# First modulations partly on VectorE, gate products of the next pair in between, stores by two queues

## The chip, the cores and the metric

The kernel runs on one core of a Trainium2 chip. The metric is device time in microseconds (us) of one execution; times of several runs are given as their median. One execution was recorded by the hardware profiler. Engines: PE is TensorE (PEld its weight loads), DVE VectorE, ACT ScalarE, POOL GpSimd, SP SyncE, which issues most DMAs.

## The reference

One layer with shared weights for 1024 latent tokens and 256 context tokens, width 1024, all in float32. `c` and `c_ctx` give nine modulation vectors each (shift, scale, gate for three sublayers):

```python
mods = split(silu(c) @ w_ada + b_ada, 9)
mods_c = split(silu(c_ctx) @ w_ada + b_ada, 9)
h  = ffn_sublayer(h, mods[0..2], g_ffn1, w_ffn1_in, w_ffn1_out)        # h + 0.5*gate*((silu(a)*b) @ w_out)
hc = ffn_sublayer(hc, mods_c[0..2], ...)                               # the context, the same weights
p_lat, p_ctx = project(h, ...), project(hc, ...)                       # q k v gates | o u vs ga gb
...                                                                    # mLSTM over chunks in both directions
mixed = sigmoid(ga) * (y_a @ w_a) + sigmoid(gb) * (y_b @ w_b)
h = h + mods[5] * (mixed @ w_o)
h = ffn_sublayer(h, mods[6..8], g_ffn2, w_ffn2_in, w_ffn2_out)
out = rmsnorm(h, g_final)
```

Each sublayer's input is `rmsnorm(h, g) * (1 + scale) + shift`.

## The kernel before

A float32 operand is split into two fp32r halves, hi (a cast on ScalarE, L143) and lo (a subtraction on VectorE, L144), and each product is three matmuls: hi hi, hi lo, lo hi. The large products of the latent stream save further by schemes of seven products where a plain block product needs eight (classes Gate, Out and others); they need sums of weight blocks and of activation blocks ahead of the products, on GpSimd (`presum`, L355 and L356, L371 to L374) and VectorE.

A scheduler in the builder sets the order of each engine's instructions; it starts from the order of the code and may let a step pass another whose buffer comes free later. Steps that are off the main line are put in a list `todo`; after each group of matmuls `pump` takes from it as many steps as the credit of the issued columns pays for. A step costs 512 unless it says otherwise, and an empty step `nop` is a way to let time pass. Buffers come from pools by a tag; a new tile of a tag takes the place of an older one and waits for the last reader of that. Tags `pg0` and `pg1` have eight pages each and serve one stage after the other.

The start: `vec`, a first part of `cst`, 32 pages of `w_ada` and `hc` (the context, two loads) are issued by SyncE in one row. The first two modulations (shift and scale of the first FFN) are computed in four quarters of 256 columns. Quarter qt holds the two slices d = 2qt and 2qt+1 of each modulation; `ada_mm` accumulates it by eight matmuls (tile adr), `ada_out` copies the row, turns it into columns (adc) and adds the bias (mods), and `scale_mod` gives smod. `nct` is the norm of the context: squares, `rstd` (p, then 11 small steps rs_x, rs_y, rs_z and diag), `bcast` (rb, a matmul that spreads the rows) and per d `mod0` (nt, hnc). Then come 22 blocks f of the context's first FFN, with two weight loads (raw, halves hl) per block, 24 matmuls pa and 24 pb each. In the first ten of them the latent stream is loaded (h), gets its position term (`add_pos`), is stored (hsp) and its squares are summed (acc on VectorE; p, L201, on TensorE). Later modulations are computed on VectorE: L751 multiplies a page by a scalar and adds, STREAM_TRANSPOSE (adtr) and TENSOR_REDUCE (adred) sum over partitions.

`Gate` computes the first half of an FFN for the latent stream: products 1 to 7 of each block pair f, in the order of `self.steps`. `head` pairs (three) run interleaved ahead of the others (order HSEQ, the last one is p=3), the other pairs overlap by two. A product of one pair over 512 columns is 12 matmuls (qa or qb by fa, fb or fc, and ring, the ring of split weights). The copy `p<-qa` (L404) and the steps L406 to L438 take the products out.

The merge: `load_split` and `last_y` put y_b and y_a into pages yp, `w_b` and `w_a` use them, fin_a forms m (gt<-gt,pt L1933, then m L1934), and the split of m is mx, in pages `pg{tb}`, for w_o. SyncE loads the next FFN's weights (rawh) meanwhile, and B.head starts their sums.

At the end `put` scales the normed output, on GpSimd where `pool_`, else on VectorE, and each result is stored at once (L1986).

Of the kernel before, what the change touches and what calls it, by code (L numbers as in the profile page):

```python
# [23 lines left out]
NKT = D // 128  # L24
# [31 lines left out]
def _build(ctx, tc, nc, a, out):  # L56
# [48 lines left out]
    class Weights:  # L105
# [10 lines left out]
        def load(self):  # L116
            n, i, w = self.order.popleft()
            src = a[n][i]
            if self.n % 4 < 2:
                raw = self.pool.tile([128, w], F32, name="raw", tag="raw", bufs=2)  # L120
            else:
                raw = hnp.tile([128, w], F32, name="raw", tag="pg1", bufs=8)
            self.n += 1
            nc.sync.dma_start(raw, src)
            hl = self.pool.tile([128, 2, w], F32R, name="hl", tag="hl", bufs=3)
            split(hl, raw)
            self.ready.append((n, i, hl))
            self.held += 1
# [44 lines left out]
    def wk(hl, k, w=128, o=0):  # L173
        return hl[:, 0, o + k * w:o + (k + 1) * w], hl[:, 1, o + k * w:o + (k + 1) * w]

    def proj(pt, wl, pgs, first):
        mm3(pt, [wk(wl, k) + (pgs[k][:, 0, :], pgs[k][:, 1, :]) for k in range(NKT)], first)

# [137 lines left out]
    class Gate:  # L316


        def __init__(self, name, raw, ring, depth, sums, pairs, head):
            self.name, self.raw, self.ring, self.depth, self.sums, self.pairs = name, raw, ring, depth, sums, pairs  # L320
            fs = [f for kp in range(pairs) for f in (kp, kp + pairs)]
            self.head = fs[:head]
            self.steps = [(f, p) for p in HSEQ for f in self.head]
            rest = fs[head:]
            for n, f in enumerate(rest):
                g = rest[n - 1]
                if not n:
                    self.steps += [(f, p) for p in (1, 2, 6, 5, 7)]
                else:
                    self.steps += [(f, 1), (f, 5), (g, 4), (f, 6), (g, 3)]  # L330
                    self.steps += [(f, p) for p in ((7, 2) if f == rest[-1] else (2, 7))]
# [465 lines left out]

    def ada_pages(qt):
        pages = []
        for kp in range(NKT // KP):  # L800
            pg = hnp.tile([128, KP, 2, QW], F32, name="adapg", tag=f"pg{1 - qt // 2}", bufs=8)
            for i in range(KP):
                src = a["w_ada"][kp * KP + i].rearrange("p (m c) -> p m c", m=9)[:, 0:2, qt * QW:(qt + 1) * QW]
                nc.sync.dma_start(pg[:, i], src)
            pages.append(pg)
        return pages

    def ada_mm(pages):
        pr = sm_ps("adr")
        for k in range(NKT):  # L810
            T.matmul(pr[0:2, 0:2 * QW], sc2[:, :, k], pages[k // KP][:, k % KP].rearrange("p m c -> p (m c)"),  # L811
                     start=k == 0, stop=k == NKT - 1)
        return pr

    def ada_out(qt, pr):
# [7 lines left out]
        for q in range(2):  # L823
            V.tensor_add(mods[:, 0:2, q, sl],
                         pc[:, 0:4 * QD].rearrange("p (m d q) -> p m d q", m=2, q=2)[:, :, :, q], bv[:, 0:2, sl])
            scale_mod(0, 1, q, "g_ffn1", sl)

    smod = cp.tile([128, 3, 2, 8], F32, name="smod")
# [34 lines left out]
    for _ in range(10):  # L863
        T.matmul(junk[:, 0:128], ones, ones, start=True, stop=True)
    apg = [ada_pages(0)]
    load_c(hcp, 4)
    for qt in (1, 2, 3):
        apg.append(ada_pages(qt))
    nc.sync.dma_start(cst[:, 1:], a["cst"].rearrange("p (a b) -> p a b", a=5)[:, 1:])
    nc.sync.dma_start(pos, a["pos"])  # L870
    hncp = [fxpage("hnc", F32R, (128, 2, 2, 256)) for _ in range(4)]
# [5 lines left out]

    prs = [ada_mm(apg[0])]
    for d in range(NKT):
        nct.sq(d)  # L880
    prs.append(ada_mm(apg[1]))
    nct.rstd()
    for qt in range(NQ):
        ada_out(qt, prs[qt])
        if qt < 2:
            prs.append(ada_mm(apg[qt + 2]))
        if qt == 0:
            nct.bcast()
        if qt:
            W.load()  # L890
        for d in range(qt * QD, (qt + 1) * QD):
            mod0(d)

# [8 lines left out]
    for f in range(NF):  # L902
        if f < NKT:
            for tb in range(2):
                nc.sync.dma_start(h[tb][f], a["xT"][f, :, tb * 512:(tb + 1) * 512])
        if 2 <= f < 2 + NKT:
# [474 lines left out]
    hnc = [fl("hnc", "hnc", (128, 2, 256), F32R, 8) for _ in range(NKT)]  # L1381
    nct.queue(smod[:, 1, 1, :], mods[:, 3, 1, :], hnc, gap=(1, 2, 12), cost=1280)
    nkq = pair_steps(("wk", emit_kq(ksp, 8), emit_kc), ("wq", emit_kq(qsp, 0)))
# [356 lines left out]
    def load_split(dst, src, tb, k):  # L1740
        r_ = t2("ld")
        nc.sync.dma_start(r_, src[tb, k])
        dst[tb][k] = hnpage(k // 4, "yp")
        split(dst[tb][k], r_)
# [124 lines left out]
    def last_y(hf, ct, sg):  # L1869
        ya[hf][ct] = hnpage(ct // 4, "yp")  # L1870
        split(ya[hf][ct], sg)
# [105 lines left out]
    n1_ = n3[1]  # L1977
    B.gate([n1_.rstd] + [nop] * 3 + [n1_.bcast] + B.F.late(fpage, lambda k: [lambda: n1_.inplace(k, m7, m6)]))

    def put(n_, tb, d, pool_, cs=slice(0, 512)):  # L1980
# [3 lines left out]
        else:  # L1984
            V.scalar_tensor_tensor(o_, o_, vc("g_final", d), n_.rb, ALU.mult, ALU.mult)
        nc.sync.dma_start(out[d, :, tb * 512 + cs.start:tb * 512 + cs.stop], o_)  # L1986

# [106 lines left out]
```

## Time and profile before

| | us |
|---|---|
| median of 3 runs | 2686.34 (2681.06 to 2689.07) |
| profiled execution | 2682.41 |
| its span | 2680.3 |
| VectorE busy | 1916.7 (72%) |
| ScalarE busy | 1141.7 (43%) |
| GpSimd busy | 440.6 (16%) |
| mean DMA rate | 170 GB/s |

The chain of work that ended last is 89% TensorE, 6% VectorE, 2% issue and 1% DMA. TensorE's idle time is thus what an edit can change, unless it changes the number of matmuls. In rows of the timeline a bracket gives the idle time of the engine just before the row and what ended it; `xN` is the number of instructions that stand in one row.

### The profile page before, as it was taken

To read this page: it belongs to the slowest core of one execution; us is meant where nothing else is said; L and a number is where in the kernel's file an instruction comes from. 1 tells how busy PE (TensorE), PEld (TensorE's weight loads), DVE (VectorE), ACT (ScalarE), POOL (GpSimd) and SP (SyncE) were. 2 spreads that over 40 slices of the span, in tenths; PEclk is the share of its full clock that TensorE was granted. 3 is DMA by queue.
4 is the path that set the end of the run, shared out by engine and by line. 5 is a ranking of instruction groups with operands and counts; after the bars stand their busy time and mean duration, and the time that the engine had idled before them with its cause. 6 is when DMAs were issued, how large, how long until landed. Compare 5 with 4: busy or idle time off the path is not lost.

```text
span 2680.3 us, 35678 instructions
## 1 busy us (share of the span) xinstructions
PE 2650.2 (99%) x12754; PEld 2210.3 (82%) x12754; DVE 1916.7 (72%) x3243; ACT 1141.7 (43%) x1952; POOL 440.6 (16%) x422
## 2 busy tenths in 40 slices
PE   9999999999999999999999999999999999999998
PEld 5998888888889878888888888888887788888887
DVE  4897688686979646687664868677568766675855
ACT  4664444344336525564443443121245444344432
POOL 0041333220000210000002005342102323230000
PEclk9999999999999999999999999999999999999999
DMA  8842344369578222356553467448140332337645
GB/s 299 315 173 99 142 165 149 114 217 327 156 254 281 85 79 86 106 169 199 194 176 105 140 238 268 166 167 279 58 159 24 126 140 99 135 122 274 201 157 173
DMA packets 202240, 456.73 MB, mean 170 GB/s; under 512 B 20432, under 2 KB 54480, under 8 KB 202064
## 3 DMA queue, kind: packets, MB, share of 16 engines
q1 hardware_dynamic: 202064, 454.47, 49.6%
q8 instruction: 100, 1.64, 0.3%
q14 instruction: 76, 0.62, 0.1%
HBM read 328.95 MB, written 125.51 MB: 170 GB/s over the span
## 4 chain that ended last, share of the span: by engine, by line
PE 89%; DVE 6%; issue 2%; DMA 1%; ACT 1%; SPq 0%; POOL 0%; POOLq 0%; ACTq 0%; DVEq 0%
PE pq L1240 17%; PE qa L389 17%; PE po L508 14%; PE qb L389 12%; PE pt L1719 9%; PE pr L1159 6%; PE pc L1030 2%; PE pn L1832 2%; PE pu L1559 2%; PE pa L169 1%; PE pb L169 1%; PE pkc L1219 1%; PE adr L811 1%; PE pn L1830 1%; DVE h L292 1%
## 5 line engine op out<-in xcount | busy, mean ns | idle before, releaser
L144 DVE TENSOR_TENSOR ring<-rawq,ring 128x512 fp32r<-128x512 f32 x408 | 310.6, 762 | 204.9 <-ACT ring L143 202.2
L508 PE MATMUL po<-gring,wring 128*128 128x512 f32 (+1 forms) x1896 | 425.1, 385 | 0.5 <-DMA gring<-fsp 0.5
L508 PEld LDWEIGHTS po<-gring,wring 128*128 128x128 f32 x1896 | 349.5, 188 | 71.9 <-issue 1.0
L143 ACT CAST ring<-rawq 128x512 fp32r<-128x512 f32 x408 | 252.9, 621 | 299.5 <-PE pq L1240 82.1
L389 PE MATMUL qa<-fc,ring 128*128 128x512 f32 x1056 | 252.6, 390 | 2.3 <-DVE ring L144 1.4
L389 PEld LDWEIGHTS qa<-fc,ring 128*128 128x128 f32 x1056 | 198.1, 188 | 44.2 <-DVE ring L144 1.8
L1240 PE MATMUL pq<-fc,ring 128*128 128x512 f32 x864 | 207.8, 393 | 0.0
L143 ACT CAST wring<-rw 128x512 fp32r<-128x512 f32 x154 | 95.9, 622 | 228.3 <-PE po L508 220.9
L1240 PEld LDWEIGHTS pq<-fc,ring 128*128 128x128 f32 x864 | 161.6, 188 | 33.3
L1719 PE MATMUL pt<-yp,ring 128*128 128x512 f32 x768 | 183.9, 396 | 1.2 <-ACT ug L1297 1.2
L144 DVE TENSOR_TENSOR wring<-rw,wring 128x512 fp32r<-128x512 f32 x154 | 106.3, 691 | 93.9 <-ACT wring L143 93.7
L1719 PEld LDWEIGHTS pt<-yp,ring 128*128 128x128 f32 x768 | 144.2, 188 | 30.7 <-ACT ug L1297 1.4
L1240 PE MATMUL pq<-fa,ring 128*128 128x512 f32 x576 | 142.3, 395 | 0.0
L1240 PE MATMUL pq<-fb,ring 128*128 128x512 f32 x576 | 138.2, 394 | 0.0
L389 PE MATMUL qa<-fb,ring 128*128 128x512 f32 x528 | 128.6, 394 | 3.7 <-ACT p L404 3.7
L389 PE MATMUL qa<-fa,ring 128*128 128x512 f32 x528 | 127.7, 391 | 1.2 <-DVE ring L144 0.7
L389 PE MATMUL qb<-fb,ring 128*128 128x512 f32 x528 | 126.8, 390 | 1.2 <-DVE p L406 0.6
L1240 PEld LDWEIGHTS pq<-fb,ring 128*128 128x128 f32 x576 | 107.7, 188 | 23.7 <-issue 0.2
L389 PE MATMUL qb<-fa,ring 128*128 128x512 f32 x528 | 126.2, 389 | 0.0
L389 PE MATMUL qb<-fc,ring 128*128 128x512 f32 x528 | 126.2, 389 | 0.0
L751 DVE SCALAR_TENSOR_TENSOR adacc<-adapg,sc,adacc 128x512 f32<-128x512 f32 x140 | 111.4, 814 | 20.1 <-DMA adapg<-in_w_ada_dram 19.3
L1240 PEld LDWEIGHTS pq<-fa,ring 128*128 128x128 f32 x576 | 106.9, 188 | 22.5 <-DVE ring L144 0.2
(342 smaller groups left out, 4803.9 us busy)
## 6 DMA issues: line engine op xcount, KB each, us to landing
adapg<-in_w_ada_dram SPq DMA_DIRECT2D x144, 256.0 KB, 3.7
fsp<-fhl SPq DMA_DIRECT2D x66, 512.0 KB, 2.6
gring<-fsp SPq DMA_DIRECT2D x66, 512.0 KB, 4.2
raw<-in_w1i_dram SPq DMA_DIRECT2D x44, 512.0 KB, 5.5
graw<-fsp SPq DMA_DIRECT2D x88, 256.0 KB, 3.6
rawq<-in_w1i_dram SPq DMA_DIRECT2D x38, 512.0 KB, 3.4
rawq<-in_w2i_dram SPq DMA_DIRECT2D x38, 512.0 KB, 3.6
fsp<-p SPq DMA_DIRECT2D x66, 256.0 KB, 2.1
```

Source lines behind the costliest of these rows:

```text
L143: S.copy(hl[:, 0, :], src)
L144: V.tensor_sub(hl[:, 1, :], src, hl[:, 0, :].bitcast(F32))
L169: T.matmul(pt, x, y, start=first and i == 0, stop=i == n - 1, skip_group_check=True)
L389: T.matmul(pt, hl[:, x, sl], pages[p][k][:, y, :], start=first and i == 0, stop=i == 11, skip_group_check=not first)
L508: T.matmul(pt[:, cs], w[:, x, sl], g[:, y, cs], start=grp and kp == 0 and i == 0, stop=kp == NFP - 1 and i == 2, skip_group_check=not grp)
L751: eng.scalar_tensor_tensor(acc, pgt, sc2[:, q, k:k + 1], acc, ALU.mult, ALU.add)
L1030: T.matmul(pt, hl[d // 4][:, x, sl], g[:, y, :], start=f == 0 and d % 2 == 0 and i == 0, stop=f == NF - 1 and i == 2, skip_group_check=True)
L1159: T.matmul(self.pt[m], pg[:, x, sl], hl[:, y, :], start=first and k == 0 and i == 0, stop=k == 3 and i == 2, skip_group_check=not first)
L1240: T.matmul(pt, hl[:, x, k * 128:(k + 1) * 128], pg[k][:, y, :], start=first and k == 0 and i == 0, stop=k == 3 and i == 2, skip_group_chec ...
L1559: T.matmul(pu[:, 0:257], ksl[:, kt * 128:(kt + 1) * 128], wv, start=True, stop=True)
L1719: T.matmul(pt, hl[:, x, k * 128:(k + 1) * 128], pg[:, y, :], start=kh + k + i == 0, stop=kh == 1 and k == 3 and i == 2)
L1832: T.matmul(pn[:, 0:257], qi[:, c_, :], self.C[d][:, c_, :], start=False, stop=c_ == 1)
```

## The change

Start: quarter 3 (d=6,7) is summed on VectorE (`ada_side`, accumulators adacc, transposes, reduces, a small matmul), the others stay on TensorE. Its pages are loaded in turn with those of quarter 1, and quarter 2's come last. The product of the context's FFN goes through k in the order 0,1,2,3,6,7,4,5. Most of `cst` and all of `pos` are loaded after the first weight loads, each h one block later. Gates: products 1, 2 and 6 of the first pair after the heads stand between the heads' products 3. Three counts of empty steps change, pages pg0 and pg1 of y_a and y_b are exchanged, and the last three results of GpSimd are stored by ScalarE's queue.

```diff
     def proj(pt, wl, pgs, first):
-        mm3(pt, [wk(wl, k) + (pgs[k][:, 0, :], pgs[k][:, 1, :]) for k in range(NKT)], first)
+        mm3(pt, [wk(wl, k) + (pgs[k][:, 0, :], pgs[k][:, 1, :]) for k in (0, 1, 2, 3, 6, 7, 4, 5)], first)
...
-            self.steps = [(f, p) for p in HSEQ for f in self.head]
+            self.steps = [(f, p) for p in HSEQ[:-1] for f in self.head]
             rest = fs[head:]
+            last = [(f, 3) for f in self.head]
             for n, f in enumerate(rest):
                 g = rest[n - 1]
                 if not n:
-                    self.steps += [(f, p) for p in (1, 2, 6, 5, 7)]
+                    for p in (1, 2, 6):
+                        self.steps += [(f, p), last.pop(0)]
+                    self.steps += last + [(f, 5), (f, 7)]
...
+    def ada_side(qt, accs):
+
+        bv = vs_("b_ada").rearrange("p (m d) -> p m d", m=9)
+        cs = slice(qt * QD, (qt + 1) * QD)
+        p8 = mm_ps("p8")
+        for q, acc in enumerate(accs):
+            red = cp.tile([128, 32], F32, name="adred", tag="adred", bufs=4)
+            ada_red(acc, red, 0)
+            T.matmul(p8[:, q * 16:q * 16 + 16], grp4, red[:, 0:16], start=True, stop=True)
+        for q in (1, 0):
+            for r in range(4):
+                sl = slice(32 * r, 32 * r + 32)
+                V.tensor_add(mods[sl, 0:2, q, cs],
+                             p8[sl, q * 16:q * 16 + 16].rearrange("p (m d r) -> p m d r", m=2, r=4)[:, :, :, r], bv[sl, 0:2, cs])
+            scale_mod(0, 1, q, "g_ffn1", cs)
...
-    apg = [ada_pages(0)]
+    apg = ada_pages((0,))
     load_c(hcp, 4)
-    for qt in (1, 2, 3):
-        apg.append(ada_pages(qt))
-    nc.sync.dma_start(cst[:, 1:], a["cst"].rearrange("p (a b) -> p a b", a=5)[:, 1:])
-    nc.sync.dma_start(pos, a["pos"])
+    apg += ada_pages((1, 3))
+    nc.sync.dma_start(cst[:, 1], a["cst"][:, 128:256])
+    apg += ada_pages((2,))
...
-    prs = [ada_mm(apg[0])]
+    pr0 = ada_mm(apg[0], range(NKT))
     for d in range(NKT):
         nct.sq(d)
-    prs.append(ada_mm(apg[1]))
+    sides = [t2("adacc") for _ in range(2)]
+    for k in range(NKT):
+        for q in range(2):
+            ada_acc(V, sides[q], ada_page(apg[2], k), q, k, k == 0)
+    pr1 = ada_mm(apg[1], range(4))
     nct.rstd()
...
+    ada_out(0, pr0)
+    ada_mm(apg[1], range(4, NKT), pr1)
+    nct.bcast()
+    for d in (0, 1):
+        mod0(d)
+    ada_out(1, pr1)
+    W.load()
+    pr2 = ada_mm(apg[3], range(NKT))
+    for d in (2, 3):
+        mod0(d)
+    ada_side(3, sides)
+    W.load()
+    for d in (6, 7):
+        mod0(d)
+    ada_out(2, pr2)
+    W.load()
+    nc.sync.dma_start(pos, a["pos"])
+    nc.sync.dma_start(cst[:, 2:], a["cst"].rearrange("p (a b) -> p a b", a=5)[:, 2:])
+    for d in (4, 5):
+        mod0(d)
...
-        if f < NKT:
+        if 0 < f <= NKT:
             for tb in range(2):
-                nc.sync.dma_start(h[tb][f], a["xT"][f, :, tb * 512:(tb + 1) * 512])
+                nc.sync.dma_start(h[tb][f - 1], a["xT"][f - 1, :, tb * 512:(tb + 1) * 512])
...
-    nct.queue(smod[:, 1, 1, :], mods[:, 3, 1, :], hnc, gap=(1, 2, 12), cost=1280)
+    nct.queue(smod[:, 1, 1, :], mods[:, 3, 1, :], hnc, gap=(1, 2, 8), cost=1280)
...
-        dst[tb][k] = hnpage(k // 4, "yp")
+        dst[tb][k] = hnpage(1 - k // 4, "yp")
...
-        ya[hf][ct] = hnpage(ct // 4, "yp")
+        ya[hf][ct] = hnpage(1 - ct // 4, "yp")
...
-    B.gate([n1_.rstd] + [nop] * 3 + [n1_.bcast] + B.F.late(fpage, lambda k: [lambda: n1_.inplace(k, m7, m6)]))
+    B.gate([n1_.rstd] + [nop] * 5 + [n1_.bcast] + B.F.late(fpage, lambda k: [lambda: n1_.inplace(k, m7, m6)]))
...
-        nc.sync.dma_start(out[d, :, tb * 512 + cs.start:tb * 512 + cs.stop], o_)
+        q = nc.scalar if pool_ and cs.stop == 512 else nc.sync
+        q.dma_start(out[d, :, tb * 512 + cs.start:tb * 512 + cs.stop], o_)
```

What the rows of an engine look like around four of these places follows; line numbers of the kernel after are larger by up to 38.

TensorE of the kernel before, blocks eight to eleven of the context's first FFN (pa and pb are 24 matmuls of one block each); p_1109 and p_1145 are the sums of squares of the latent stream's two halves, L201:

```order
L169 MATMUL pa<-hnc,hl 128x256 x24
L169 MATMUL pb<-hnc,hl 128x256 x24
L169 MATMUL pa<-hnc,hl 128x256 x6
L201 MATMUL p_1109<-ones,acc 128x1 x4
L169 MATMUL pa<-hnc,hl 128x256 x12
L201 MATMUL p_1145<-ones,acc 128x1 x4
L169 MATMUL pa<-hnc,hl 128x256 x6
L169 MATMUL pb<-hnc,hl 128x256 x24
```

TensorE of the kernel after, from the same block on (there p_1129 and p_1165):

```order
L169 MATMUL pa<-hnc,hl 128x256 x24
L201 MATMUL p_1129<-ones,acc 128x1 x4
L201 MATMUL p_1165<-ones,acc 128x1 x4
L169 MATMUL pb<-hnc,hl 128x256 x24
L169 MATMUL pa<-hnc,hl 128x256 x24
L169 MATMUL pb<-hnc,hl 128x256 x6
L214 MATMUL rb<-diag,ones 128x512
L169 MATMUL pb<-hnc,hl 128x256 x8
```

VectorE of the kernel after at the same place; the first hl is that of the ninth block's pa, the second that of its pb:

```order
L144 TENSOR_TENSOR hl<-raw,hl 128x1024
L196 TENSOR_TENSOR acc<-acc,sq 128x512 x2
L885 TENSOR_TENSOR h<-h,pos 128x512
L196 TENSOR_TENSOR acc<-acc,sq 128x512
L722 TENSOR_SCALAR rs_x<-p_1129 128x4
L722 TENSOR_SCALAR rs_x<-p_1165 128x4
L727 TENSOR_SCALAR rs_y<-rs_x 128x4
L144 TENSOR_TENSOR hl<-raw,hl 128x1024
```

The matmuls L201 have moved ahead by more than a block and stand between pa and pb, and the hl for that pb stands behind the two rs_x that read them.

TensorE of the kernel before in the first FFN's gate: the end of the heads (qb<-fc x36 are their three products 3) and the next pair:

```order
L389 MATMUL qa<-fc,ring 128x512 x72
L389 MATMUL qb<-fc,ring 128x512 x36
L389 MATMUL qa<-fa,ring 128x512 x12
L389 MATMUL qb<-fa,ring 128x512 x12
L389 MATMUL qa<-fb,ring 128x512 x12
L389 MATMUL qb<-fb,ring 128x512 x12
```

TensorE of the kernel after, from the same row on:

```order
L392 MATMUL qa<-fc,ring 128x512 x72
L392 MATMUL qa<-fa,ring 128x512 x12
L392 MATMUL qb<-fc,ring 128x512 x6
L392 MATMUL qb<-fa,ring 128x512 x12
L392 MATMUL qb<-fc,ring 128x512 x6
L392 MATMUL qa<-fb,ring 128x512 x4
L392 MATMUL qb<-fc,ring 128x512 x2
L392 MATMUL qa<-fb,ring 128x512
L392 MATMUL qb<-fc,ring 128x512 x4
L392 MATMUL qa<-fb,ring 128x512 x7
L392 MATMUL qb<-fc,ring 128x512 x9
```

The 36 products qb<-fc that stood ahead of the pair now stand in pieces between its products.

VectorE of the kernel before, between the last products of w_a and the first of w_o; mx_17008 (not shown) to mx_17029 in steps of 3 are the eight k of tb=0, mx_17032 and on those of tb=1:

```order
L144 TENSOR_TENSOR mx_17032<-m_16436,mx_17032 128x512
L144 TENSOR_TENSOR mx_17035<-m_16437,mx_17035 128x512
L144 TENSOR_TENSOR mx_17038<-m_16438,mx_17038 128x512
L1933 TENSOR_TENSOR gt_16987<-gt_16987,pt_16948 128x512
L144 TENSOR_TENSOR mx_17041<-m_16439,mx_17041 128x512
L1934 TENSOR_TENSOR m_16443<-m_16443,gt_16987 128x512
L144 TENSOR_TENSOR mx_17044<-m_16440,mx_17044 128x512
L1933 TENSOR_TENSOR gt_17004<-gt_17004,pt_16961 128x512
L144 TENSOR_TENSOR mx_17029<-m_16443,mx_17029 128x512
```

VectorE of the kernel after at the same place; mx_17027 to mx_17048 are now the eight k of tb=0:

```order
L144 TENSOR_TENSOR mx_17027<-m_16455,mx_17027 128x512
L144 TENSOR_TENSOR mx_17030<-m_16456,mx_17030 128x512
L144 TENSOR_TENSOR mx_17033<-m_16457,mx_17033 128x512
L1971 TENSOR_TENSOR gt_17006<-gt_17006,pt_16967 128x512
L144 TENSOR_TENSOR mx_17036<-m_16458,mx_17036 128x512
L1972 TENSOR_TENSOR m_16462<-m_16462,gt_17006 128x512
L144 TENSOR_TENSOR mx_17039<-m_16459,mx_17039 128x512
L1971 TENSOR_TENSOR gt_17023<-gt_17023,pt_16980 128x512
L144 TENSOR_TENSOR mx_17042<-m_16460,mx_17042 128x512
L1972 TENSOR_TENSOR m_16462<-m_16462,gt_17023 128x512
L144 TENSOR_TENSOR mx_17045<-m_16461,mx_17045 128x512
L144 TENSOR_TENSOR mx_17048<-m_16462,mx_17048 128x512
```

Before, seven of tb=0's casts are through ahead of these rows and only the eighth stands among tb=1's; after, all eight of tb=0 stand here and seven of tb=1 are ahead of them.

## Rows read from the trace of the kernel before

**Rows 1.** The page's first part: busy time, share of the span, instructions.

```profile
PE 2650.2 (99%) x12754; PEld 2210.3 (82%) x12754; DVE 1916.7 (72%) x3243; ACT 1141.7 (43%) x1952; POOL 440.6 (16%) x422
```

**Rows 2.** Waits of TensorE: what waited, releaser, us in total, times, longest.

```profile
PE qa L389 <- ACT p L404: 3.7, 2, 2.3
PE rb L214 <- DVE diag L210: 2.9, 2, 1.8
...
PE pt L1719 <- ACT ug L1297: 1.2, 1, 1.2
PE pb L169 <- DVE hl L144: 1.0, 3, 0.4
...
PE pvc L1318 <- DVE nt L225: 0.8, 1, 0.8
```

**Rows 3.** Timeline of TensorE: start us, us, instructions; the start.

```profile
15.24 8.72 PE L811 MATMUL adr<-adapg,sc 128*2 128x512 f32 x16 [2.51 <-DMA adapg<-in_w_ada_dram]
...
41.91 1.69 PE L169 MATMUL pa<-hnc,hl 128*128 128x256 f32 x12
...
50.91 3.04 PE L169 MATMUL pa<-hnc,hl 128*128 128x256 f32 x24
```

**Rows 4.** Steps of VectorE: a group, a tile's durations (ns), two timeline rows.

```profile
L751 DVE SCALAR_TENSOR_TENSOR adacc<-adapg,sc,adacc 128x512 f32<-128x512 f32 x140 | 111.4, 814 | 20.1 <-DMA adapg<-in_w_ada_dram 19.3
...
L755 DVE STREAM_TRANSPOSE adtr<-adacc x20: 667/704/717, 338.5 to 1406.9; 128x512 f32<-128x512 f32 x20
...
13.72 3.61 DVE L196 TENSOR_TENSOR acc<-acc,sq 128x256 f32<-128x256 f32 x7 [13.72 <-ACT sq L195]
...
37.81 2.36 DVE L144 TENSOR_TENSOR hl<-raw,hl 128x1024 fp32r<-128x1024 f32 x2 [0.38 <-ACT hl L143]
```

**Rows 5.** Two windows: busy us of PE, PEld, DVE, ACT, POOL; PEclk, DMA share, GB/s.

```profile
15.00:20.00 5.00, 4.76 (x8) 0.83 (x9) 1.92 (x5) 1.26 (x4) 0.00 (x0) 0.66 1.09 348
2030.00:2066.00 36.00, 34.45 (x149) 27.29 (x147) 35.79 (x50) 26.28 (x46) 8.33 (x5) 1.00 0.00 1
```

**Rows 6.** Timeline of VectorE and TensorE around the sums of squares.

```profile
98.03 1.89 DVE L196 TENSOR_TENSOR acc<-acc,sq 128x512 f32<-128x512 f32 x3
...
101.44 3.04 PE L169 MATMUL pb<-hnc,hl 128*128 128x256 f32 x24
...
105.19 0.95 PE L201 MATMUL p<-ones,acc 128*128 128x1 f32 x8
...
106.26 1.22 DVE L144 TENSOR_TENSOR hl<-raw,hl 128x1024 fp32r<-128x1024 f32 x1
```

**Rows 7.** Timeline, first FFN's gate, the first pair after the heads.

```profile
237.30 2.88 PE L389 MATMUL qa<-fa,ring 128*128 128x512 f32 x12
...
243.67 0.58 ACT L404 COPY p<-qa 128x512 f32<-128x512 f32 x1
...
244.30 3.06 PE L389 MATMUL qa<-fb,ring 128*128 128x512 f32 x12 [1.40 <-ACT p L404]
```

**Rows 8.** Timeline, second FFN's gate, heads and the pair after them.

```profile
2067.05 10.76 PE L389 MATMUL qa<-fc,ring 128*128 128x512 f32 x46 [1.42 <-DVE ring L144]
...
2085.81 2.88 PE L389 MATMUL qa<-fa,ring 128*128 128x512 f32 x12
...
2093.08 0.57 ACT L404 COPY p<-qa 128x512 f32<-128x512 f32 x1
...
2093.70 4.61 PE L389 MATMUL qa<-fb,ring 128*128 128x512 f32 x12 [2.29 <-ACT p L404]
```

**Rows 9.** The end of w_a: three timeline rows and a window.

```profile
1931.59 1.78 DVE L1934 TENSOR_TENSOR m<-m,gt 128x512 f32<-128x512 f32 x1
...
1935.00 0.67 DVE L1933 TENSOR_TENSOR gt<-gt,pt 128x512 f32<-128x512 f32 x1
...
1936.82 3.92 PE L1719 MATMUL pt<-mx,ring 128*128 128x512 f32 x16 [0.89 <-DVE mx L144]
...
1927.00:1938.00 11.00, 10.11 (x45) 8.07 (x44) 11.00 (x10) 4.79 (x8) 9.64 (x6) 1.00 0.28 95
```

**Rows 10.** The output's stores: durations in ns, first and last start us.

```profile
L1986 SPq DMA_DIRECT2D out_dram<-h x16: 332/398/414, 2665.7 to 2677.6; - x16
```

More of the change, by code (lines that the diff above doesn't have):

```diff
@@ L121, in load @@
             else:
-                raw = hnp.tile([128, w], F32, name="raw", tag="pg1", bufs=8)
+                raw = hnp.tile([128, w], F32, name="raw", tag="pg0" if self.n == 2 else "pg1", bufs=8)
             self.n += 1
@@ L796, in _build, with ada_pages, ada_page, ada_mm @@
     KP = 512 // QW
-    def ada_pages(qt):
-        pages = []
+    def ada_pages(qts):
+        res = [[] for _ in qts]
         for kp in range(NKT // KP):
[L801 to L812, printed above, removed]
+            for pages, qt in zip(res, qts):
+                pg = hnp.tile([128, KP, 2, QW], F32, name="adapg", tag=f"pg{1 - qt // 2}", bufs=8)
+                for i in range(KP):
+                    src = a["w_ada"][kp * KP + i].rearrange("p (m c) -> p m c", m=9)[:, 0:2, qt * QW:(qt + 1) * QW]
+                    nc.sync.dma_start(pg[:, i], src)
+                pages.append(pg)
+        return res
+    def ada_page(pages, k):
+        return pages[k // KP][:, k % KP].rearrange("p m c -> p (m c)")
+    def ada_mm(pages, ks, pr=None):
+        if pr is None:
+            pr = sm_ps("adr")
+        for k in ks:
+            T.matmul(pr[0:2, 0:2 * QW], sc2[:, :, k], ada_page(pages, k), start=k == 0, stop=k == NKT - 1,
+                     skip_group_check=True)
         return pr
@@ L876, in mod0 @@
         nct.mod(d, smod[:, 0, 1, :], mods[:, 0, 1, :], hnc[d][:, 0, :], hnc[d][:, 1, :])
-    prs = [ada_mm(apg[0])]
+    pr0 = ada_mm(apg[0], range(NKT))
     for d in range(NKT):
         nct.sq(d)
-    prs.append(ada_mm(apg[1]))
-    nct.rstd()
[L883 to L892, printed above, removed]
+    sides = [t2("adacc") for _ in range(2)]
[3 more added lines that the diff above has]
+    pr1 = ada_mm(apg[1], range(4))
+    nct.rstd()
+    ada_out(0, pr0)
[18 more added lines that the diff above has]
+        mod0(d)
     n1 = [Norm(h[tb], 512, V) for tb in range(2)]
```

## The prediction

> **What bounds the kernel now.** I read the shares of the span first: TensorE is busy 2650.2 of 2680.3 us [rows 1], so at most 30 us can be won by closing gaps, and the change takes no work from the 128x512 matmuls that fill the rest. Next the list of waits of TensorE [rows 2]: the reader is to see that no releaser costs more than 4 us in the whole run. Each edit must therefore be judged at one place of the timeline, where I read the matmul row with a bracket (its idle time) and then what ScalarE, VectorE and GpSimd did just before it. 0.3% is about 8 us; a smaller difference can't be told from no change by measuring this kernel.
>
> **The change part by part.** The sum is made against the profiled execution, 2682.4 us (span 2680.3 and 2.1 around it), which lies 3.9 us under the median of 2686.3; I carry the difference over to the median. Gains are positive.
>
> *The start, +2.4.* TensorE's work on the four quarters starts its last three at 15.24 and reaches the first products at 41.91, and the second block of the first FFN at 50.91 [rows 3]; 24 products of 128x256 make a row of 3.04, so the first block's 48 would need some 6 and took 9.0, because its operands come late. The change puts the quarter d=6,7 on VectorE: two multiplies and 14 multiply-adds, 0.81 us each in the mean of the 140 later ones [rows 4], some 11.5 if I take 0.72, since GpSimd is idle here. They start at 17.3, when the sum of squares ends [rows 4]; the rstd steps between them (11 of 0.2) give 31. Then mods and nt/hnc of the first two quarters (3.5), two transposes of 0.70 [rows 4] and two reduces about as long: 37.3 to 38.3. Three hl of 1.2 [rows 4] and the small steps of the other quarters (5.5) give 46.4 to 47.7, and TensorE begins its second block at 47.2 to 48.5: 2.4 to 3.7 earlier. I take the lower end, because the queue that loads is full here. VectorE becomes the longer engine in this stretch, so TensorE idles while it waits for diag (about 28.5) and for the reduces. After an idle stretch before 15.24 the granted clock was 0.66 [rows 5], the mean of time at 1.2 and at 2.4 GHz; three passes stood 0.855 us apart instead of 0.43, which is 1.3 us for one such fall. The products of quarter 2 end at 36.7, 0.6 to 1.6 before the reduces, so a fall costs 0 to 0.7. Bounds 0.5 to 3.7.
>
> *The norm of the latent stream, -2.1.* The h loads come one block later, but the sums of squares over partitions (L201) now stand in the ninth block, between its pa and its pb; before they stood inside the pa of the tenth, with the sum done at 99.9 and the matmuls at 105.2 [rows 6]: five us of slack. Behind L201 on VectorE's queue now stands the hl that the ninth block's pb needs. So TensorE ends L201, VectorE does two rs_x and an rs_y (0.3) and the hl (1.2) [rows 6], and only then do products go on: 1.5 lost. The last acc is due at about 102.0 of the old scale, TensorE at 101.4 [rows 6] plus 0.3 for its own late hl: 0.3. Then the rs chain (1.7), the next hl, gc and diag (0.9) stand on VectorE in one line, and each rb waits for its diag: 0.2 and 0.6. Together 2.6. Against that, the stalls by hl at 92.3 (pa) and 95.8 (pb, among the 1.0 of the list [rows 2]), 1.1 together, should halve, as an h load less stands before each raw: +0.5. Bounds -3.3 to +1.0.
>
> *The pairs of the gates, +1.4 and +3.2 and +1.2.* In FFN1 the first qa<-fb of the next pair waits 1.40 for a copy of qa that ScalarE reaches at 243.67 and ends at 244.25 [rows 7]; qa was complete at 240.2, and one product of 2.72 stands between. Now two such stretches stand there (qb<-fc x6, qb<-fa x12, qb<-fc x6), 5.44: the matmul is ready at 245.6, after the copy even if that stays where it is. +1.4 (0 to 1.4). In FFN2 the same wait is 2.29, and the 12 matmuls behind it take 4.61 instead of 2.88, 1.73 more [rows 8]. The copy ended 4.95 us after qa, 0.5 under 5.44, so the 2.29 goes; of the 1.73, which is a late VectorE, I take half: 3.2 (2.3 to 4.0). The sums of the next pair move on GpSimd from 2059.6 to 2006, when it is idle. There they stretched VectorE's steps (as [rows 9] show of another place) and TensorE waited 1.42 for a ring [rows 8]. That wait goes; its neighbour is the next one: five GpSimd sums instead of three fall at 2068 to 2085, so I take 1.2 (-0.5 to 1.4).
>
> *The two more empty steps before bcast, 0.* The wait of rb for diag, 1.1 of the 2.9 in the list [rows 2], goes, but VectorE is busy for 35.8 of the 36 us from 2030 to 2066 [rows 5] and is what the next products wait for; the time turns up there. Bounds -0.3 to 1.1.
>
> *Four fewer empty steps ahead of the context's modulations, +0.8.* They start four steps, 2.7 us, earlier, and pvc waits 0.8 for nt [rows 2]; VectorE has pauses there. 0 to 0.9.
>
> *The swapped pages, 0 and -2.8.* For yb the first products still wait on ug, which stands on ScalarE behind casts that wait for loads: 1.2 stays [rows 2]. For ya the swap reaches further: the pages of mx for tb=0 are now those whose last reader is w_a's last product, so VectorE casts tb=1 first, and six of tb=0's eight after that product has begun. GpSimd works on sums for 9.6 of the 11 us from 1927 to 1938 [rows 9]. A VectorE step with two inputs from SBUF then takes 1.78 (m), while gt, with one from PSUM, keeps 0.67 [rows 9]. With the durations of these rows, tb=0's k4 to k7 come out at 1935.1, 1936.8, 1939.0 and 1939.7, where TensorE, which starts this product at 1930.78, wants one each 0.68 us from 1933.5 on: stalls of 1.6, 1.0 and 1.6 less what overlaps, 3.9 in all, and 1.1 before [rows 9]. -2.8 (-4 to 0).
> The Trainium skill, SBUF — State Buffer, "SBUF: two separate sides", says that the port pair that VectorE and GpSimd share is an exclusive lock for a whole instruction, taken by a VectorE operation with two SBUF inputs; this agrees with 1.78 against 0.67, and it speaks against the order above. By it a step could wait for a whole sum of 1.6 before its own 0.7, an estimate of 2.3 instead of 1.78, and the term would be -5 instead of -2.8.
>
> *The last stores, +1.3.* SyncE issues 16 stores of 0.33 to 0.41 us, and the last one starts at 2677.6 [rows 10], two us after the last result. Three go to ScalarE's queue, which is idle: three slots of about 0.45. Bounds 0.5 to 1.5.
>
> Sum: 2.4 - 2.1 + 1.4 + 3.2 + 1.2 + 0 + 0.8 - 2.8 + 1.3 = 5.4, so 2677.0 for the profiled execution and 2680.9 on the median. (With the skill's price for the pages it would be 2683.)
>
> **The rivals.**
> A. The forecast, 2680.9. For it: each stall and each new wait is one that the order of instructions shows.
> B. The two new waits don't come: DMAs bring h early enough that the ninth block's hl is only a few tenths late, and GpSimd's sums don't meet the mx casts, as they start on a release that moves with them. Then 5.4 + 2.1 + 2.8 = 10.3, and up to 13.6 with the upper ends of start, gates and hl: 2676 (2673 at best). Against it: the hl stands behind L201 on one in-order queue, which no early load mends.
> C. The gates give nothing: VectorE is the late engine in both (72% busy over the run, 35.8 of 36 us from 2030 to 2066), so the waits turn up at the next products. 5.4 - 1.4 - 3.2 - 1.2 = -0.4: 2686.7. Against it: the copy of qa is late because of its place in ScalarE's queue, and TensorE is given other work until then.
> D. Slower: the start of w_o. If all 12 VectorE steps up to tb=0's k7 take 1.78, that one is done at 1948.3, where TensorE wants it at 1935.5: a stall of 12.8, 11.7 more than before, against 8.2 from all other terms: 3.5 slower, 2689.8. It decides from a stall of 9.3 at this place on. Against it: GpSimd has six sums there, 10 us, so that only some six steps can be stretched.
>
> **How the numbers follow.** A 0.45 (own range 2677 to 2685), B 0.30, C 0.13, D 0.12. A fifth of A and nearly all of B lie over 8 us faster: 0.37. Over 8 us slower are half of D and a share of C in which the start loses too: 0.10. The rest, 0.53, is within 0.3%. The range runs from B with most of its upper ends, 2671, to D, 2690.
>
> **What would show it.** In the profile after: pa of the second block at 47.2 to 48.5; the ninth block's pb behind L201 with a bracket of 1 to 2 us and hl as releaser, and rb brackets after it; no bracket on qa<-fb at the first pair of either gate; pvc without its 0.8; brackets by mx of 3 to 4 us in all at the first product of w_o; the last store starting about 1.3 earlier. Wrong would be the forecast if TensorE's idle time in all falls by more than 9 or by less than 2 us, or if the products themselves change their pace (0.2267 us for one of 128x512).

## The result, and the profile after

The changed kernel took 2689.26 us (median of 20 runs, 2685.63 to 2694.13), the kernel before 2683.1 (20 runs on the same chip): a ratio of 1.002 with an interval of 1.0013 to 1.0026. That is 5.4 us slower by the ratio, less than the 0.3% set as a bound, but on the other side of zero from the 5.4 us gain that was forecast. The profiled execution took 2686.24 (span 2684.5), 3.8 more than that of before.

The page's first part of the changed kernel, against [rows 1]:

```profile
PE 2646.1 (99%) x12734; PEld 2208.9 (82%) x12734; DVE 1934.8 (72%) x3269; ACT 1143.0 (43%) x1951; POOL 442.6 (16%) x422
```

TensorE is busy 4.1 us less while the span is 4.2 longer, so its idle time has grown by 8.3 us, from 30.1 to 38.4. The list of its waits (what waited, releaser, us in total, times, longest) says where; lines 330 to 790 of before stand three lower down, later ones 9 to 39:

```profile
PE qa L392 <- DVE y L418: 6.6, 4, 4.2
PE adr L820 <- DMA adapg<-in_w_ada_dram: 5.4, 5, 2.5
PE pt L1757 <- DVE mx L144: 3.3, 3, 1.3
PE rb L214 <- DVE diag L210: 2.9, 2, 1.8
PE pa L169 <- DVE hl L144: 1.9, 2, 1.4
PE pb L169 <- DVE hl L144: 1.8, 2, 1.1
PE pt L1757 <- ACT ug L1335: 1.6, 1, 1.6
```

The 3.7 us of waits for the copy p, first in [rows 2], are gone, and so is pvc's 0.8. In their place stands qa for y, 6.6 us, which before was this:

```profile
PE qa L389 <- DVE y L415: 0.9, 1, 0.9
```

The waits for mx have come as forecast (3.3 in all), and rb's wait is 2.9 as it was.

A single execution scatters by some 3 us, so I also read each stage by the time at which the same matmul stands in both traces, before and behind the stage. Against the profile of before, in us of the changed kernel (plus is lost): start to 51 us, -4.98; from there to 205, with the norm of the latent stream, +3.17; first gate, +1.2; modulations of the context, -1.07; 990 to 1012, +1.56; start of w_o, +2.47; second gate, +0.54; all up to 2660 together, +5.01, and the span's end, behind the stores, +4.2. What is missing to 5.01 (2.1) lies in stages that the change doesn't touch.

The changed kernel's side quarter on VectorE and its stores, for [rows 4, 10] (durations in ns, least, median, most; first and last start us):

```profile
L754 DVE SCALAR_TENSOR_TENSOR adacc<-adapg,sc,adacc x14: 744/747/750, 17.9 to 28.6; 128x512 f32<-128x512 f32 x14
...
L2025 SPq DMA_DIRECT2D out_dram<-h x21: 332/383/449, 2654.0 to 2680.8; - x21
...
L2025 ACTq DMA_DIRECT2D out_dram<-h x3: 338/338/413, 2679.2 to 2680.6; - x3
```

Timeline of TensorE in the changed kernel (start us, us, instructions; a bracket is idle time and its releaser), at the start, at the sums of squares and in the two gates, for [rows 3, 6, 7, 8]:

```profile
45.93 3.04 PE L169 MATMUL pa<-hnc,hl 128*128 128x256 f32 x24
...
97.01 1.84 PE L201 MATMUL p<-ones,acc 128*128 128x1 f32 x16
...
100.31 4.14 PE L169 MATMUL pb<-hnc,hl 128*128 128x256 f32 x22 [1.08 <-DVE hl L144]
...
295.73 3.01 PE L392 MATMUL qa<-fc,ring 128*128 128x512 f32 x12 [1.47 <-DVE y L418]
...
2098.50 2.88 PE L392 MATMUL qa<-fc,ring 128*128 128x512 f32 x12
2101.22 2.88 PE L392 MATMUL qa<-fa,ring 128*128 128x512 f32 x12
2103.94 2.88 PE L392 MATMUL qb<-fb,ring 128*128 128x512 f32 x12
2106.66 1.07 PE L392 MATMUL qa<-fb,ring 128*128 128x512 f32 x4
2111.90 5.39 PE L392 MATMUL qa<-fc,ring 128*128 128x512 f32 x12 [4.18 <-DVE y L418]
```

The last line is the new wait. A bank qa takes products 1, 6, 7 and 4 of one pair; product 4 must not begin before VectorE has read product 7 out of the bank (`y<-y,qa`). Product 7 was complete at 2101.4 (the first of these rows from 2098.50 on: 2098.50 + 2.88), product 4 is the last row. VectorE came to its read of product 7 ten us later; its timeline there:

```profile
2106.13 1.77 DVE L425 TENSOR_TENSOR u<-u,y 128x512 f32<-128x512 f32 x1
2107.83 1.75 DVE L441 TENSOR_TENSOR ft<-u,p 128x512 f32<-128x512 f32 x1
2109.50 1.75 DVE L144 TENSOR_TENSOR fhl<-u,fhl 128x512 fp32r<-128x512 f32 x1
2111.17 0.68 DVE L418 TENSOR_TENSOR y<-y,qa 128x512 f32<-128x512 f32 x1
```

What stands ahead of y are the last steps of the third head: the sum of its product 3 and the outputs. Three of these took 1.75 to 1.77 instead of the 0.68 of other steps here, beside sums on GpSimd (1.59 to 1.83 each from 2103.44 to 2110.70); that is 3.2 us more, against a wait of 4.18. No run takes these sums away, so their share of the wait is an estimate. Windows of the changed kernel (busy us of PE, PEld, DVE, ACT, POOL with counts, granted clock, DMA share, GB/s), two stages of 16 us and the stretch of the wait:

```profile
2080.00:2096.00 16.00, 15.96 (x70) 12.26 (x69) 6.68 (x10) 6.60 (x12) 1.87 (x2) 1.00 0.05 17
2096.00:2112.00 16.00, 11.82 (x53) 9.47 (x51) 15.86 (x20) 9.95 (x18) 8.25 (x5) 0.94 0.23 82
2111.00:2115.00 4.00, 3.10 (x7) 2.48 (x8) 3.86 (x7) 0.97 (x2) 0.00 (x0) 0.50 0.61 240
```

and the same two stages before:

```profile
2080.00:2096.00 16.00, 13.71 (x58) 10.99 (x57) 15.86 (x22) 8.40 (x16) 4.93 (x3) 0.95 0.21 71
2096.00:2112.00 16.00, 16.00 (x68) 13.10 (x67) 9.64 (x12) 6.33 (x12) 5.84 (x4) 0.94 0.48 176
```

The change leaves VectorE idle for over half of the first stage, in which the products 3 come late, and puts its work into the second, where it has 0.14 us free. The granted clock fell to 0.50 behind the wait (1.2 GHz, half of full speed): 12 matmuls took 5.39 instead of 2.88.

### The profile page after: what moved, and what is told of

The parts are those of the page before. It is cut to its first block, busy times and chain, and to the rows that moved or that the text cites. A ratio compares the mean times of both kernels' runs of the same rounds, so it can differ in the third digit from the quotient of the medians.

```text
span 2684.5 us, 35656 instructions
## 1 busy us (share of the span) xinstructions
PE 2646.1 (99%) x12734; PEld 2208.9 (82%) x12734; DVE 1934.8 (72%) x3269; ACT 1143.0 (43%) x1951; POOL 442.6 (16%) x422
## 4 chain that ended last, share of the span: by engine, by line
PE 86%; DVE 6%; issue 3%; DMA 3%; ACT 1%; SPq 0%; POOL 0%; POOLq 0%; DVEq 0%; ACTq 0%
PE pq L1278 17%; PE qa L392 16%; PE po L511 14%; PE qb L392 11%; PE pt L1757 9%; PE pr L1197 6%; PE pc L1068 2%; PE pn L1870 2%; PE pu L1597 2%; PE pb L169 1%; PE pa L169 1%; DMA adapg<-in_w_ada_dram 1%; PE pkc L1257 1%; PE pn L1868 1%; DVE ring L144 1%
## 5 line engine op out<-in xcount | busy, mean ns | idle before, releaser
L754 DVE SCALAR_TENSOR_TENSOR adacc<-adapg,sc,adacc 128x512 f32<-128x512 f32 x154 | 121.8, 812 | 19.8 <-DMA adapg<-in_w_ada_dram 18.7
```

What stands on the lines that cost most here:

```text
L754: eng.scalar_tensor_tensor(acc, pgt, sc2[:, q, k:k + 1], acc, ALU.mult, ALU.add)
```

## The experiments

In the expectations T is the theory and the R's are its rivals; what each says stands there. The ratio is to the kernel before on the same chip, with its 95% interval; the stage figures are read as above. The edits are to the changed kernel unless another is named.

**The gates' old order.**

```diff
-            self.steps = [(f, p) for p in HSEQ[:-1] for f in self.head]
-            last = [(f, 3) for f in self.head]
+            self.steps = [(f, p) for p in HSEQ for f in self.head]
...
-                    for p in (1, 2, 6):
-                        self.steps += [(f, p), last.pop(0)]
-                    self.steps += last + [(f, 5), (f, 7)]
+                    self.steps += [(f, p) for p in (1, 2, 6, 5, 7)]
```

> The changed kernel with the gate products in the old order (self.steps as before), all else as changed. Theory T: the new order takes away the waits for the copy of qa but pushes the three heads' last steps (u, p, ft, fhl) on VectorE into the next pair, where y waits behind them; the first gate is 1.2 us longer by it in the profile after, the second 0.5. T expects 1 to 3 us faster than the changed kernel (ratio to the kernel before about 1.001), the wait of qa for y L418 of 4.2 us gone, and the waits for p L407 of 1.4 and 2.3 back. Rival R1 (the new order is worth its 4 to 6 us and the loss lies elsewhere) expects 4 to 6 us slower than the changed kernel, ratio about 1.004.

2689.4, 1.0015 (1.0006 to 1.0024). The waits are back where they were (waits of TensorE):

```profile
PE qa L389 <- ACT p L404: 4.5, 2, 3.1
...
PE qa L389 <- DVE y L415: 0.8, 1, 0.8
```

First gate -0.16, second -1.29, where the changed kernel had +1.2 and +0.54: 3.2 us better in the gates by the stages, though the time doesn't tell this kernel from the changed one. So the gates' new order is no gain, and the loss is not in the gates alone.

**The old pages.**

```diff
-        dst[tb][k] = hnpage(1 - k // 4, "yp")
+        dst[tb][k] = hnpage(k // 4, "yp")
...
-        ya[hf][ct] = hnpage(1 - ct // 4, "yp")
+        ya[hf][ct] = hnpage(ct // 4, "yp")
```

> The changed kernel with the pages of y_a and y_b as before. T: the waits of w_o's first product for mx, 3.3 us in the profile after, go back to about 1; 2.5 us faster than the changed kernel, ratio about 1.001. Rival R2 (GpSimd's sums make these waits whatever the page order, and the exchange is free): no difference, waits for mx of 3 us stay.

2685.76, 1.0007 (0.9998 to 1.0016). The start of w_o stands at +0.01 against +2.47: the pages cost there what the trace showed.

**The last squares one block later.**

```diff
-                slow(n1[tb].sq, f - 2)
+                if f < 1 + NKT:
+                    slow(n1[tb].sq, f - 2)
...
         if f == 2 + NKT:
+            for tb in range(2):
+                slow(n1[tb].sq, NKT - 1)
```

> The changed kernel, but the squares of the latent stream's last slice (d=7) are queued one block of the context's FFN later, so that the sums over partitions (L201) stand in the tenth and eleventh block, and hl is ahead of them on VectorE. T: the wait of pb for hl behind L201 (1.1 in the profile after, and 22 matmuls of 128x256 in 4.1 instead of 2.9, because the clock fell) goes; 2.5 to 3 us faster than the changed kernel, ratio about 1.001. Rival R3 (the loss of the start's gain at 100 us comes from late loads, DMA share 1.0 there): the waits move by a block and 0 to 0.5 us are gained.

2693.0, 1.0032 (1.002 to 1.0044); the stretch to 205 lost 4.70. The wait behind L201 went, and another stands in its place. Timeline of this kernel at the ninth block:

```profile
101.48 1.04 ACT L143 CAST hl<-raw 128x1024 fp32r<-128x1024 f32 x1 [4.92 <-DMA raw<-in_w1i_dram]
...
102.58 0.50 PE L169 MATMUL pb<-hnc,hl 128*128 128x256 f32 x2 [1.40 <-ACT hl L143]
```

The weights (raw) come late here, and ScalarE waits 4.92 for them. This theory fell: with h loaded late, moving L201 away wins nothing.

**One product of the next pair between the heads' last.**

```diff
-                    for p in (1, 2, 6):
-                        self.steps += [(f, p), last.pop(0)]
-                    self.steps += last + [(f, 5), (f, 7)]
+                    self.steps += [last[0], last[1], (f, 1), last[2], (f, 2), (f, 6), (f, 5), (f, 7)]
```

> The changed kernel with another order in the gates: two of the heads' last products come before the next pair and only the third between its products 1 and 2 (24 matmuls instead of 12 between qa's product 1 and 6, as in the changed kernel). T: the waits for the copy of qa stay away (both) and VectorE has two of the three heads' last steps done before; the waits for y L418 shrink to under 2 us in all; 3 to 6 us faster than the changed kernel, ratio about 1.000. R1: as the changed kernel. If the waits for y stay at 4 us, their cause is GpSimd's sums beside VectorE's steps, not the place of the heads' products.

2683.04, 0.9993 (0.9985 to 1.0002). First gate -1.7, second -3.4; no wait for p, and one for y of 0.8. One product 3 behind the pair's product 1 is enough to cover the copy, and with the two others ahead of the pair VectorE gets its work early.

**The loads of h as before.**

```diff
-        if 0 < f <= NKT:
+        if f < NKT:
             for tb in range(2):
-                nc.sync.dma_start(h[tb][f - 1], a["xT"][f - 1, :, tb * 512:(tb + 1) * 512])
+                nc.sync.dma_start(h[tb][f], a["xT"][f, :, tb * 512:(tb + 1) * 512])
```

> The changed kernel, but each h is loaded in the same block as before instead of one later. In five profiles with the changed start TensorE begins the second block 1.2 to 5.0 us earlier than before, and 2.8 to 6.2 us are lost again between 85 and 168 us; queueing the last squares a block later (the run with L201 moved) did not bring them back, and hl waited for raw there. Theory T2: late h loads hold up SyncE's queue (the store of h, hsp, waits for h ahead of raw), so with the old loads the stretch from 85 to 168 loses at most 2 us and the start keeps at least 1 of its gain: 2 us faster than the changed kernel. Rival R4: DMAs are full from 75 to 105 either way, and the loss stays at 3 to 6 us: no difference.

2689.88, 1.0012 (1.0003 to 1.0022). From 85 to 121 us it lost 1.0 against before, where the seven kernels with the late h lose 2.8 to 5.4, and from 85 to 168 2.0 against 3.0 to 6.2 (T2 has at most 2, R4 3 to 6); the time doesn't show it (the changed kernel had 1.002).

**One product between, and the old pages** (both edits above).

> The changed kernel with the gate order of the run with one product in between (ratio 0.9993) and the pages of y_a and y_b as before (alone 2.5 to 4 us, as the wait for mx went). T: the two add up, ratio 0.998 (5 us faster than the kernel before). Rival: with less waiting at w_o the second gate's VectorE work comes no earlier, and 2 of the 4 us come back as waits there: ratio 0.999.

2679.09, 0.9972 (0.9961 to 0.9982). First gate -1.7, second -3.4, start of w_o +0.04: the two edits add up, as T says.

**The kernel before with one product between, the four fewer empty steps and the two store queues.**

```diff
-            self.steps = [(f, p) for p in HSEQ for f in self.head]
+            self.steps = [(f, p) for p in HSEQ[:-1] for f in self.head]
+            last = [(f, 3) for f in self.head]
...
-                    self.steps += [(f, p) for p in (1, 2, 6, 5, 7)]
+                    self.steps += [last[0], last[1], (f, 1), last[2], (f, 2), (f, 6), (f, 5), (f, 7)]
...
-    nct.queue(smod[:, 1, 1, :], mods[:, 3, 1, :], hnc, gap=(1, 2, 12), cost=1280)
+    nct.queue(smod[:, 1, 1, :], mods[:, 3, 1, :], hnc, gap=(1, 2, 8), cost=1280)
...
-        nc.sync.dma_start(out[d, :, tb * 512 + cs.start:tb * 512 + cs.stop], o_)
+        q = nc.scalar if pool_ and cs.stop == 512 else nc.sync
+        q.dma_start(out[d, :, tb * 512 + cs.start:tb * 512 + cs.stop], o_)
```

> The kernel before with three edits alone: the gate order with one product in between, four fewer empty steps ahead of the context's modulations, and the last stores on two queues; start, loads and pages as before. T: by the stages of the profiles -1.7 (first gate), -3.4 (second), -1.1 (modulations) and -0.8 (stores): 7 us faster than the kernel before, ratio 0.9974. If the start is worth its 2.6 us, the run with all edits but pages (f2) is not slower than this one; T expects it slower by 1 to 2 us, because 85 to 168 loses more than the start gains.

2678.76, 0.9973 (0.9962 to 0.9984). The whole gain of the previous kernel is there with the old start, so the new start is not needed for it; that it costs 1 to 2 us, as T has it, doesn't show.

**One product between, old pages, h as before.**

> As the run with one product in between and old pages, and h loaded in the same block as before. T2: 2 us faster than that one, ratio 0.9973. R4: the same as that one, 0.998.

2677.24, 0.9965 (0.9953 to 0.9978), the lowest of all and better than both kernels; against the two previous ones the intervals overlap. Its second gate, timeline of TensorE:

```profile
2091.66 2.88 PE L390 MATMUL qa<-fb,ring 128*128 128x512 f32 x12
2094.38 2.88 PE L390 MATMUL qb<-fb,ring 128*128 128x512 f32 x12
2097.10 2.88 PE L390 MATMUL qa<-fc,ring 128*128 128x512 f32 x12
2099.82 2.88 PE L390 MATMUL qa<-fa,ring 128*128 128x512 f32 x12
2102.54 2.88 PE L390 MATMUL qb<-fb,ring 128*128 128x512 f32 x12
2105.26 2.88 PE L390 MATMUL qa<-fc,ring 128*128 128x512 f32 x12
```

its VectorE and its two stages:

```profile
2100.14 1.77 DVE L144 TENSOR_TENSOR fhl<-ft,fhl 128x512 fp32r<-128x512 f32 x1
2101.83 0.68 DVE L416 TENSOR_TENSOR y<-y,qa 128x512 f32<-128x512 f32 x1
```

```profile
2080.00:2096.00 16.00, 15.85 (x70) 13.03 (x71) 15.19 (x22) 10.65 (x20) 3.87 (x3) 1.00 0.20 67
2096.00:2112.00 16.00, 16.00 (x72) 13.28 (x71) 11.10 (x13) 6.28 (x11) 8.61 (x4) 1.00 0.56 206
```

No bracket on qa<-fb, none on product 4 at 2105.26: y is done at 2102.5, 2.7 before it is needed. VectorE works 15.19 of the first 16 us and has 4.9 to spare in the second.

**The kernel before with the changed gate order alone** (the first diff, the other way).

> The kernel before with the changed gate order alone (products 1, 2 and 6 of the next pair between the heads' products 3). The forecast gave this edit -5.8 us (first gate -1.4, second -4.4). T: VectorE gets all three heads' last steps after the next pair's products have begun, the adds y<-y,qa stand behind them, and TensorE waits at product 4; by the stages of four profiles +2.2 in the first gate (1.2 to 3.5) and +0.4 in the second (-0.2 to 0.9): 1 to 4 us slower than the kernel before, ratio 1.001. Rival R1: the gate loses only together with the changed start or pages: 4 to 6 us faster, ratio 0.998.

2688.49, 1.0015 (1.0006 to 1.0023): the new order by itself is slower, by 4.0 us (1.6 to 6.2). Timeline of TensorE, first and second gate:

```profile
297.24 4.61 PE L392 MATMUL qa<-fc,ring 128*128 128x512 f32 x12 [2.22 <-DVE y L418]
...
2112.32 4.55 PE L392 MATMUL qa<-fc,ring 128*128 128x512 f32 x12 [4.22 <-DVE y L418]
```

Both have the wait for y, and behind both the clock fell (12 matmuls 4.61 and 4.55 instead of 2.88).

**The fastest kernel with two products between.**

```diff
-                    self.steps += [last[0], last[1], (f, 1), last[2], (f, 2), (f, 6), (f, 5), (f, 7)]
+                    self.steps += [last[0], (f, 1), last[1], (f, 2), last[2], (f, 6), (f, 5), (f, 7)]
```

> The fastest kernel so far (one product in between, old pages, h loaded as before) with two heads' products moved behind the next pair's first one: the first head's product 3, pair's 1, second head's, pair's 2, third head's, pair's 6. T: with two heads' last steps late on VectorE some of the wait for y comes back: 0.5 to 3 us slower than that kernel, ratio 0.997 to 0.998. If GpSimd's sums make the wait and not the number of late heads, it is the same as with one.

2677.63, 0.9974 (0.9965 to 0.9984): not told apart from one product. The longest wait for y is 1.3. So the loss comes between this order and the changed one, in which all three products 3 stand behind the pair's product 1 and the third behind its product 6; which of the two differences decides was not tried.

**The kernel before with the changed start alone** (its core; with it `ada_side`, the two pages in turn, and the order of the product).

```diff
-        if f < NKT:
+        if 0 < f <= NKT:
             for tb in range(2):
-                nc.sync.dma_start(h[tb][f], a["xT"][f, :, tb * 512:(tb + 1) * 512])
+                nc.sync.dma_start(h[tb][f - 1], a["xT"][f - 1, :, tb * 512:(tb + 1) * 512])
...
-    prs.append(ada_mm(apg[1]))
+    sides = [t2("adacc") for _ in range(2)]
+    for k in range(NKT):
+        for q in range(2):
+            ada_acc(V, sides[q], ada_page(apg[2], k), q, k, k == 0)
+    pr1 = ada_mm(apg[1], range(4))
```

> The kernel before with the changed start alone (quarter 3 on VectorE, the order of loads, h one block later); gates, empty steps, pages and stores as before. T: the gain at the second block (1.2 to 5.0 us in six profiles, mean about 3) is lost again by 205 us (2.8 to 6 between 85 and 168): -1 to +2 us, ratio 0.9996 to 1.0008. Rival: the start keeps the forecast +2.4 us where nothing else is changed: ratio 0.999.

2685.45, 1.000 (0.9992 to 1.0009). Gain at the start and loss behind it cancel. It also tells of the second gate, which is unchanged here:

```profile
2095.51 3.02 PE L389 MATMUL qa<-fb,ring 128*128 128x512 f32 x12 [2.29 <-ACT p L404]
```

This is the wait of [rows 8], as long to the hundredth, but the 12 matmuls behind it took 3.02, not 4.61, and its granted clock from 2096 to 2100 was 1.00. The kernel with the gates' old order, the first of these experiments, has a longer wait there and no slower matmuls either:

```profile
2100.15 3.06 PE L389 MATMUL qa<-fb,ring 128*128 128x512 f32 x12 [3.09 <-ACT p L404]
```

**The kernel before with the exchanged pages alone** (the second diff, the other way).

> The kernel before with the pages of y_a and y_b exchanged alone. The forecast gave this 2.8 us slower (0 to 4). T: the step of the profiles between 1925 and 1960 us, +2.5 to +4.15 with exchanged and 0.0 to 0.06 with old pages: 3 to 4 us slower, ratio 1.0013. Rival R2 (the step needs the changed gate, whose sums start on GpSimd in the same stretch): 0 to 1 us, ratio 1.000.

2689.12, 1.0011 (1.0001 to 1.002): 3.0 us, with an interval from 0.3 to 5.4; the start of w_o +4.09. So the pages' loss does not need the other edits. Timeline of TensorE there:

```profile
1934.84 0.96 PE L1719 MATMUL pt<-mx,ring 128*128 128x512 f32 x3 [0.73 <-DVE mx L144]
1938.21 27.98 PE L1719 MATMUL pt<-mx,ring 128*128 128x512 f32 x115 [2.40 <-DVE mx L144]
```

## Why the prediction was wrong

The parts measured alone make up the result: gate order +4.0, pages +3.0, start 0.0 by time, and by stages -1.07 for the empty steps and -0.8 for the stores. That is 5.1, and 5.4 was measured; with intervals of 1.6 to 6.2 for the gates, 0.3 to 5.4 for the pages and some 2 either way for the start, so close a sum is luck.

**The gates, +1.4, +3.2 and +1.2 forecast, a loss of 4.0 measured.** This is the step that failed. Its first half was right: both copy waits went. It then asked only whether qa would be ready for that pair's product 6, the first that waits for the copy. The next use of VectorE on that bank, the read of product 7 ahead of product 4, was not followed, though the steps of the heads that had been moved stand ahead of it in VectorE's queue. Rival C named VectorE as the late engine and still priced the gates at nothing; they cost. Rival D's time, 2689.8, is near the measured one by luck: its stall of 12.8 at w_o measured 3.3. The experiments show both halves: with one product between, the gates gain 1.3 to 1.7 and 3.4 to 3.7 by the stages; with the changed order the wait for y is 4.2 in the second gate of all five kernels that have it.

The 1.73 behind the 2.29 was misread too. I called it a late VectorE; of the four profiles with the old order only that of before has it (the changed start alone 3.02 behind the same wait, the exchanged pages alone 3.02 behind 2.33, the gates' old order 3.06 behind 3.09), and in the profile of before the granted clock is 0.76 from 2096 to 2100:

```profile
2096.00:2100.00 4.00, 4.00 (x15) 3.16 (x15) 2.87 (x5) 1.74 (x3) 2.17 (x2) 0.76 0.98 339
```

It was a clock fall of that one execution, so half of it was no term. It also stands in every figure of the second gate above: two profiles without any change to that gate (the start alone, the pages alone) read -1.6 there. Against these the order with one product between gains about 2 in the second gate, not 3.4 to 3.7, and the changed order loses 1.4 (alone) to 2.1 (the changed kernel).

The ring's neighbour (+1.2) came. In the five kernels with the changed order no wait for a ring stands among the heads' products on qa, where the profiles of before, of the start alone and of the pages alone have 1.42; from 2000 us to the last of those products they gain 2.8 to 2.9 against before (the smaller waits ahead of it shrink too). What was won there was lost again behind, at y.

**The start, +2.4.** Right in size. Ten profiles with the new start reach its end 2.85 earlier in the mean than the profile of before, three without it and that profile itself 0.88, so 2.0 is the gain, an estimate good to about 1: the single ones are 0.45 to 4.98 and -0.25 to 1.95 earlier. The second block began at 45.93, before the forecast 47.2 to 48.5, but 2 us of it are scatter that unchanged code shows too.

**The norm of the latent stream, -2.1.** The mechanism is in the trace: L201 in the ninth block (counted from 0; it moved ahead by 30 matmuls, less than a block), hl on VectorE behind it at 99.03, a bracket of 1.08, and 22 matmuls in 4.14 at a granted clock of 0.80 from 102 to 105. That fall of the clock was not in the sum; of the sum's other parts, no bracket came on rb, and the stalls by hl ahead of L201 did not halve (0.48 and 0.76, before 0.67 and 0.40). From 51 to 205 us the four profiles with the old start lose 0.2 in the mean, the seven with the new start and the late h 3.8 (2.1 to 5.4), the three with the new start and h as before 1.5 (1.2 to 2.0). In these three L201 stands between the same pa and pb, but VectorE does hl ahead of rs_x, and no bracket follows; VectorE and TensorE of the fastest kernel:

```profile
98.46 1.23 DVE L144 TENSOR_TENSOR hl<-raw,hl 128x1024 fp32r<-128x1024 f32 x1 [2.28 <-ACT hl L143]
100.13 0.16 DVE L720 TENSOR_SCALAR rs_x<-p 128x4 f32<-128x4 f32 x1 [0.44 <-PE p L201]
...
99.14 1.84 PE L201 MATMUL p<-ones,acc 128*128 128x1 f32 x16
100.85 2.88 PE L169 MATMUL pb<-hnc,hl 128*128 128x256 f32 x22
```

So it is the late h that puts hl behind L201, and the argument against rival B, that no early load mends this, was wrong. The experiment that took L201 away and left h late did not win the stretch back: there the weights came late. By time, start and norm together are 0.0.

**The empty steps.** -1.0 to -1.1 in every profile that has the four fewer in the context's modulations (+0.8 forecast, pvc's wait gone); rb's wait is 2.9 as before with two more in front of bcast (0 forecast for the time, though the wait was expected to move).

**The pages, -2.8.** Right, and the size at its bounds: 2.5 in the changed kernel and 4.1 in five others where they are exchanged, 0.0 to 0.1 where not. The 1.6 between are the clock: behind the last wait for mx it was granted 1.00 in the changed kernel (1940 to 1944 us) and 0.67 with the pages alone (1938 to 1942). VectorE's `m` took 1.77 and mx 1.76 there, gt 0.67, as in [rows 9]. The step of 2.3, the prediction's estimate by the Trainium skill (SBUF — State Buffer, "SBUF: two separate sides"), did not come; the term of 5 by it neither.

**The stores, +1.3.** 0.8 to 1.0: from the end of the last matmul to the span's end it is 6.5 to 6.6 in the ten profiles with two queues and 7.3 to 7.5 in the four with one.

## What to carry to other kernels

When products are moved to cover the readout of a bank, follow that bank through all its uses, and list what the reading engine's queue then holds in front of each: an accumulating bank ties TensorE to the reader more than once. Move no more than covers the wait: here one product in between took it (two did no worse), three brought it back elsewhere. Before a stall is priced, take out of the row what the granted clock explains, and read the same row in a second execution.

## What the runs showed of the hardware

The clock does not fall behind every wait of the same length. The wait of 2.29 at the same place cost 1.7 us of slower matmuls in one execution and 0.1 in another, and one of 3.09 there cost 0.2. Behind the wait of 4.2 for y it fell in all five kernels that have it (12 matmuls took 4.53 to 5.49). It also fell where TensorE had no wait: from 994 to 998 the changed kernel was granted 0.57 and the kernel before 1.00, with TensorE busy throughout in both:

```profile
994.00:998.00 4.00, 4.00 (x14) 3.43 (x15) 0.60 (x3) 3.56 (x6) 0.00 (x0) 0.57 0.01 4
```

Six of the 14 profiles have this, and lose 1.56 to 1.61 there, among them the fastest kernel; the code is the same in all. Ahead of it stand 20 matmuls of 32x16 in 2.40 us. The Trainium skill (TensorE: Matmul & The Clock Gate, "What's actually happening") has the clock follow how busy the array was shortly before; the falls behind waits agree with it, and no run here shows why the same wait, or the same narrow matmuls, do it in some executions only.
